# Both column halves of the second feed-forward product by seven-product slabs, two streams in the same seven PSUM banks

## The chip, the cores and the metric

One core of a Trainium2 chip runs the whole program in one launch. The metric is the device time of one execution in microseconds, as the median of several runs. The kernel before has 2032.6 us.

The engines are named as in the profile: PE multiplies matrices, PEld is its weight load, DVE does elementwise work with one or two tensor inputs, ACT does elementwise work with a function or a scale, POOL is a third elementwise engine that also issues DMAs, SP issues DMAs. SBUF is the on-chip memory of 128 partitions, PSUM the small accumulator memory that PE writes, in banks of 128 x 512 float32.

## What is computed

Two transformer layers over 256 tokens of width 2048, in float32. Each layer has a token mixer (pooling with memory attention in the first, differential attention with memory attention in the second) and a feed-forward block. The change is in the feed-forward block:

```python
def squared_relu_mlp(h, w1, w2):
    z = jax.nn.relu(h @ w1)
    return (z * z) @ w2
...
        x = x + squared_relu_mlp(rms_norm(x, ffn_norm[i]), w_ff1[i], w_ff2[i])
```

Here w1 is 2048 x 8192 and w2 is 8192 x 2048, so the second product sums over 8192 channels, 64 chunks of 128.

## The kernel before

**Precision.** A float32 operand is cut in two: a rounded part (hi, a cast by ACT) and the remainder (lo, a subtraction by DVE). A product of two such operands is three matmuls: hi by hi, hi by lo, lo by hi. Weights come from HBM in float32 and are cut on the way: `Feed._split` (L159) casts into `hi_ring` (L164) and subtracts into `lo_ring` (L165). The rings have six slots of 512 columns (`SLOTS`), and a slot is free again when PE has used it. Weights are prepared three jobs ahead of PE (`AHEAD`) and loaded three loads ahead of that (`LOADS`).

**Plain tiles.** `a_part` (L404) computes 128 output channels for all 256 tokens. For each 128 x 128 weight block it loads hi as PE's weights and streams 512 columns (the activations' hi and lo side by side, L418), then loads lo and streams 256 columns (L420). A tile over 16 chunks of k is 32 matmuls. Four blocks are a quad, one half of a 512 KB load (`raw`), and after each quad `tick()` runs the small work that was put off with `at(delay, ...)`.

**Slabs.** The right half of the second product's columns (1024 to 2047) goes by Winograd's form of Strassen's scheme: two chunks of k by two 512-column halves by two token halves of 128, in seven products where the plain way has eight. The seven products add into seven PSUM banks that stay open over the whole layer (`open_banks`, L848), and `finish_banks` (L853) forms the four result blocks and transposes them into the residual. A slab is four jobs (`slab_jobs`, L817; `sides` says which operands and banks): job 0 has two products, job 1 one, jobs 2 and 3 two each, 21 matmuls of 512 columns. Here the activations are PE's weights and the weight rows stream. The weight sums are made on DVE: `t1` (L192), then `rb` (L197), then `ra` (L189, 1024 columns). The activations' sums are made by `combine` (L748, L753 to L756) and cut into `sit` (L759, L762). A slab's rows are two loads of 512 KB (`slab`).

**The order of the feed-forward block.** `ffn` (L715) writes the order out by hand. Up tiles (first product, `up_tile`, L773) and down tiles (second product, left half, `down_tile`, L788) share one PSUM bank, `x_bank`; ACT copies it out (L739), DVE adds the two halves (L780) and multiplies the ReLU by the row scale r (one instruction at L781, shown at L314), ACT squares it (L784), ACT and DVE cut it into `z` (L743, L746). The 64 up tiles come in four quarters of 16; after each quarter 8 down tiles sum its 16 chunks into the residual (L799, L800), and 8 slabs take the same chunks. One slab goes to three tiles (`groups`), and its jobs stand between the tiles, so that PE has work while ACT copies `x_bank` out. The last four slabs and eight down tiles (`last`, L916) are mixed by the table `ends`.

**Loads.** All weight loads are issued by SP in the order of `Plan.loads`. For a slab, a preparing step ("K", two steps ahead of its first job, `KOFF`) makes the sums t1 and rb.

Of the kernel before, what the change touches and what calls it, by code (L numbers as in the profile page):

```python
# [17 lines left out]
P = 128  # L18
# [36 lines left out]
class Plan:  # L55
# [13 lines left out]
    def close(self):  # L69
        prep = []  # L70
        for job in self.jobs:

            late = job[0] == "S" and job[1] % 32 > 28
            if job[0] == "S" and job[2] == 0 and not late:
                prep.insert(max(0, len(prep) - KOFF), ("K", job[1]))
            if late and job[2] == 1:
                prep.append(("L", job[1]))
            prep.append(job)
# [4 lines left out]
        for p in prep:  # L83
            if p[0] == "K":
                self.loads += [("S", p[1], 0), ("S", p[1], 1)]
            elif p[0] == "L":
                self.loads.append(("S", p[1], 1))
            elif p[0] == "S" and p[2] == 0 and ("S", p[1], 0) not in self.loads:
                self.loads.append(("S", p[1], 0))
# [15 lines left out]
class Feed:  # L105


    def __init__(self, tc, wst, wpool, rows, plan, dry):
# [7 lines left out]
        self.t1 = None  # L116
        self.behind = None
# [7 lines left out]
    def load(self, upto):  # L125
        while self.lp < min(upto, len(self.plan.loads)):
# [6 lines left out]
            elif r[2] and r[1] % 32 > 29:  # L133
                t = self.spare[r[1] % 2]
            else:
                t = self.rows.tile([P, 1024], F32, tag="rows", bufs=3, name=f"slab{h}")
            self.nc.sync.dma_start(t[:, 0:n], self.wst[h, :, 0:n])
# [34 lines left out]
    def _prepare(self, p):  # L172
        sub, add = self.nc.vector.tensor_sub, self.nc.vector.tensor_add
        self.load(self.plan.need[p] + 1 + LOADS)
# [9 lines left out]
        t1 = self.t1[1 if p[1] % 32 > 28 else p[1] % 2]  # L184

        def both():
            t2 = rb[:, 0:512].unsqueeze(1).to_broadcast([P, 2, 512])
            two = ra.rearrange("p (a c) -> p a c", a=2)
            sub(two, t2, two)  # L189

        if p[0] in "KL":
            one = add(t1, ra[:, 0:512], rb[:, 0:512])  # L192
# [4 lines left out]
            sub(rb[:, 0:512], t1, rb[:, 512:1024])  # L197
            if p[0] == "L":
                both()
# [4 lines left out]
        if p[2] == 0 and ("K", p[1]) in self.plan.need:  # L204
            both()
# [71 lines left out]
def program(ctx, tc, plan, dry, xT, memT, par, lam, cst, wst, yT):  # L277
# [437 lines left out]
    def ffn(l, xs, tags, done):  # L715
# [8 lines left out]
        sit = sp.tile([P, 8, 1024], F32R, tag=tags[1], name=f"sit{l}")  # L724
        room = sp.tile([P, 6144], F32, tag="big", name=f"room{l}")
        stage = [room[:, T * j : T * j + T] for j in range(8)]
        sums = [room[:, 2048 + 512 * j : 2560 + 512 * j] for j in range(2)]

        feed.spare = [room[:, 1024 * j : 1024 * j + 1024] for j in range(2)]
        feed.t1 = [room[:, 3072 + 512 * j : 3584 + 512 * j] for j in range(2)]  # L730
        outs = [room[:, 4096 + 512 * j : 4608 + 512 * j] for j in range(3)]
        r = []
        banks = []
        cnt = [0]

        def evict(ps):
            x = outs[cnt[0] % 3]
# [4 lines left out]
        def high(j):  # L742
            nc.scalar.copy(z[:, j, 0:T], stage[j % 8])  # L743

        def low(j):
            nc.vector.tensor_sub(z[:, j, T : 2 * T], stage[j % 8], z[:, j, 0:T].bitcast(F32))  # L746

        def combine(i):  # L748

            a11, a21 = stage[2 * i % 8][:, 0:P], stage[2 * i % 8][:, P:T]  # L750
            a12, a22 = stage[(2 * i + 1) % 8][:, 0:P], stage[(2 * i + 1) % 8][:, P:T]
            s1, s2, s3, s4 = (sums[i % 2][:, c * P : c * P + P] for c in range(4))
            nc.vector.tensor_add(s1, a21, a22)  # L753
            nc.vector.tensor_sub(s3, a11, a21)
            nc.vector.tensor_sub(s2, s1, a11)
            nc.vector.tensor_sub(s4, a12, s2)  # L756

        def sums_high(i):
            nc.scalar.copy(sit[:, i, 0:512], sums[i % 2])  # L759

        def sums_low(i):
            nc.vector.tensor_sub(sit[:, i, 512:1024], sums[i % 2], sit[:, i, 0:512].bitcast(F32))  # L762

        def convert(j, d):
            at(d, lambda: high(j))
            at(d + 2, lambda: low(j))
            if j % 2:
                i = j // 2
                at(d + 3, lambda: combine(i))
                at(d + 5, lambda: sums_high(i))  # L770
                at(d + 7, lambda: sums_low(i))

        def up_tile(q, i, ps):  # L773
            a_part(ps, "w_ff1", l, q * NK + i, range(NK), xs)
            if not r:
                r.append(rstd_from("x"))
            y = evict(ps)

            def first():
                nc.vector.tensor_add(y[:, 0:T], y[:, 0:T], y[:, T : 2 * T])  # L780
                stt(y[:, 0:T], y[:, 0:T], 0.0, r[0], ALU.max, ALU.mult)  # L781

            at(1, first)
            at(3, lambda: nc.scalar.activation(stage[i % 8], y[:, 0:T], AF.Square))  # L784
            if q == 0 or i > 0:
                convert(i, 3)

        def down_tile(q, n, ps, between=None):  # L788
            end = l == 1 and q == 3 and n == 7
            if end:  # L790
                c_tile(ps, "w_ff2", l, n, range(q * NK, q * NK + NK), z)
                nc.vector.tensor_add(resid[:, n, :], resid[:, n, :], ps[:, 0:T])
# [692 lines left out]
```

## Time and profile before

| | before |
|---|---|
| median of 3 runs | 2032.6 us (2032.13 to 2032.81) |
| span of the profiled execution, first to last instruction | 2030.2 us |
| time of the profiled execution beside its span | not listed apart; the median lies 2.4 us above the span |
| ACT busy, in the stretch 600 to 800 us | 133.26 of 200 us |
| DVE busy, in the same stretch | 173.35 of 200 us |
| moved by DMA | 390.75 MB, mean 192 GB/s |
| granted clock of PE | 1.000 |

How to read it. In the list of groups a line shows the source line, the engine, the operation, output and inputs with their shapes, the count, the busy time in us and the mean duration in ns, then the idle time before these instructions and what ended it. A timeline row has the start, the duration, the engine and the instruction. The ends of matmuls are modelled, so their durations overlap; the pace of PE is read from start to start. A table of stretches has, for each, the length, the busy time of PE, PEld, DVE, ACT and POOL with the count of instructions, the granted clock, the share of the DMA engines and GB/s. The list of DMAs has the size and the time from issue to landing. The feed-forward block of the first layer runs from about 250 to 937 us, that of the second from about 1343 us to the end.

### The profile page before, as it was taken

To read this page: it belongs to the slowest core of one execution; us is meant where nothing else is said; L and a number is where in the kernel's file an instruction comes from. 1 tells how busy PE (TensorE), PEld (TensorE's weight loads), DVE (VectorE), ACT (ScalarE), POOL (GpSimd) and SP (SyncE) were. 2 spreads that over 40 slices of the span, in tenths; PEclk is the share of its full clock that TensorE was granted. 3 is DMA by queue.
4 is the path that set the end of the run, shared out by engine and by line. 5 is a ranking of instruction groups with operands and counts; after the bars stand their busy time and mean duration, and the time that the engine had idled before them with its cause. 6 is when DMAs were issued, how large, how long until landed. Compare 5 with 4: busy or idle time off the path is not lost.

```text
span 2030.2 us, 32210 instructions
## 1 busy us (share of the span) xinstructions
PE 2025.3 (100%) x11022; PEld 1744.0 (86%) x11022; DVE 1718.6 (85%) x3233; ACT 1352.6 (67%) x2537; POOL 53.5 (3%) x67
## 2 busy tenths in 40 slices
PE   9999999999999999999999999999999999999999
PEld 8888888888888888888888888888888888888888
DVE  8888889889879978999765798989879978888997
ACT  7765577666656756678665698566657656766764
POOL 0001300000000000000000000310000000000000
PEclk9999999999999999999999999999999999999999
DMA  9566556555556565655565534555555555565564
GB/s 318 167 201 190 191 176 204 191 197 198 187 198 203 185 205 195 206 178 178 187 235 191 173 122 155 188 180 200 187 198 198 187 204 194 188 213 195 193 209 135
DMA packets 110470, 390.75 MB, mean 192 GB/s; under 512 B 12512, under 2 KB 15200, under 8 KB 110304
## 3 DMA queue, kind: packets, MB, share of 16 engines
q1 hardware_dynamic: 110160, 388.68, 57.2%
q8 instruction: 86, 1.41, 0.3%
q14 instruction: 80, 0.66, 0.1%
q10 hardware_dynamic: 144, 0.01, 0.0%
HBM read 386.54 MB, written 2.10 MB: 191 GB/s over the span
## 4 chain that ended last, share of the span: by engine, by line
PE 99%; ACT 0%; DVE 0%; issue 0%
PE x_bank L418 33%; PE x_bank L420 16%; PE wo L418 6%; PE p L813 5%; PE p L814 5%; PE p L815 5%; PE wo L420 3%; PE u L418 2%; PE ff L418 2%; PE u L420 1%; PE q L452 1%; PE q L454 1%; PE k L452 1%; PE q L453 1%; PE k L454 1%; PE v L454 1%
## 5 line engine op out<-in xcount | busy, mean ns | idle before, releaser
L164 ACT CAST hi_ring<-raw 128x512 fp32r<-128x512 f32 x1193 | 736.0, 620 | 510.8 <-PE x_bank L418 302.9
L165 DVE TENSOR_TENSOR lo_ring<-raw,hi_ring 128x512 fp32r<-128x512 f32 x1193 | 816.2, 694 | 189.0 <-ACT hi_ring L164 148.9
L418 PE MATMUL x_bank<-fx,hi_ring 128*128 128x512 f32 x1920 | 601.8, 395 | 0.0
L420 PEld LDWEIGHTS x_bank<-fx,lo_ring 128*128 128x128 f32 x1920 | 360.6, 188 | 84.0
L420 PE MATMUL x_bank<-fx,lo_ring 128*128 128x256 f32 x1920 | 377.1, 278 | 0.0
L418 PEld LDWEIGHTS x_bank<-fx,hi_ring 128*128 128x128 f32 x1920 | 301.3, 189 | 9.4
L418 PE MATMUL x_bank<-z,hi_ring 128*128 128x512 f32 x960 | 300.9, 395 | 0.0
L165 DVE TENSOR_TENSOR lo_ring<-slab,hi_ring 128x1024 fp32r<-128x1024 f32 x188 | 229.9, 1223 | 54.2 <-ACT hi_ring L164 53.5
L164 ACT CAST hi_ring<-slab 128x1024 fp32r<-128x1024 f32 x188 | 196.8, 1047 | 73.3 <-PE x_bank L418 37.8
L420 PEld LDWEIGHTS x_bank<-z,lo_ring 128*128 128x128 f32 x960 | 180.3, 188 | 41.9
L420 PE MATMUL x_bank<-z,lo_ring 128*128 128x256 f32 x960 | 188.6, 278 | 0.0
L418 PE MATMUL wo<-cat,hi_ring 128*128 128x512 f32 x512 | 161.8, 397 | 0.3 <-DVE rc L389 0.3
L418 PEld LDWEIGHTS x_bank<-z,hi_ring 128*128 128x128 f32 x960 | 151.8, 189 | 6.4 <-ACT room L739 0.4
L420 PEld LDWEIGHTS wo<-cat,lo_ring 128*128 128x128 f32 x512 | 95.9, 188 | 22.0
L739 ACT COPY room<-x_bank 128x512 f32<-128x512 f32 x180 | 104.8, 582 | 2.0 <-PE x_bank L420 2.0
L420 PE MATMUL wo<-cat,lo_ring 128*128 128x256 f32 x512 | 101.5, 279 | 0.0
L813 PE MATMUL p<-hi_ring,sit 128*128 128x512 f32 x256 | 100.4, 392 | 0.0
L814 PE MATMUL p<-hi_ring,sit 128*128 128x512 f32 x256 | 100.1, 391 | 0.0
L815 PE MATMUL p<-lo_ring,sit 128*128 128x512 f32 x256 | 99.6, 389 | 0.0
L784 ACT ACTIVATE room<-room 128x256 f32<-128x256 f32 x128 | 53.2, 416 | 42.1 <-DVE room L314 41.9
L418 PEld LDWEIGHTS wo<-cat,hi_ring 128*128 128x128 f32 x512 | 78.3, 189 | 1.1 <-ACT mq L606 0.5
L813 PE MATMUL p<-hi_ring,z 128*128 128x512 f32 x192 | 75.1, 391 | 0.0
(343 smaller groups left out, 3078.2 us busy)
## 6 DMA issues: line engine op xcount, KB each, us to landing
raw<-in_w SPq DMA_DIRECT2D x596, 512.0 KB, 3.7
slab<-in_w SPq DMA_DIRECT2D x124, 512.0 KB, 3.6
memraw<-in_mem SPq DMA_DIRECT2D x5, 512.0 KB, 3.8
resid<-in_x SPq DMA_DIRECT2D x8, 256.0 KB, 5.6
room<-in_w SPq DMA_DIRECT2D x4, 512.0 KB, 5.0
out_y<-resid SPq DMA_DIRECT2D x16, 128.0 KB, 1.9
memraw<-in_mem SPq DMA_DIRECT2D x5, 256.0 KB, 5.6
memraw<-in_mem SPq DMA_DIRECT2D x2, 128.0 KB, 3.6
```

Of the source, the lines that this page charges most:

```text
L164: self.last_cast = self.nc.scalar.copy(hi, src)
L165: low = self.nc.vector.tensor_sub(lo, src, hi.bitcast(F32))
L418: nc.tensor.matmul(ps, hi, xs[:, k, :], start=first and c == 0, stop=False)
L420: nc.tensor.matmul(ps[:, T : 2 * T], lo, xs[:, k, 0:T], start=False, stop=last and c == len(ks) - 1,)
L452: nc.tensor.matmul(ps[t], x[t][1], hi, start=k == 0, stop=False)
L453: nc.tensor.matmul(ps[t], x[t][0], hi, start=False, stop=False)
L454: nc.tensor.matmul(ps[t], x[t][0], lo, start=False, stop=k == NK - 1)
L739: nc.scalar.copy(x, ps)
L784: at(3, lambda: nc.scalar.activation(stage[i % 8], y[:, 0:T], AF.Square))
L813: nc.tensor.matmul(ps, a[1], hi, start=first, stop=False)
L814: nc.tensor.matmul(ps, a[0], hi, start=False, stop=False)
L815: nc.tensor.matmul(ps, a[0], lo, start=False, stop=last)
```

## The change

1. The left half of the columns goes by slabs too, for the first 48 chunks of k: 24 more slabs in each layer. The last 16 chunks of the left half stay plain (8 down tiles).
2. There are now two streams, g = 0 (right half) and g = 1 (left half), for the same seven banks. The order is four slabs of one stream, then eight of the other, and so on. At each exchange the banks of one job are copied to SBUF by ACT, two ticks after that job's last product, and the other stream's partial sums are copied back into the bank by ACT (`swap`, `restore`); matmuls then add onto them. After the last slab of the left half its result blocks are formed at once (`close_left`) and transposed into the residual by four `turn_left`.
3. Up tiles run one after another from 4 to 63 with no down tiles between. `due` puts slab jobs before each tile and after each of its quads by a table of due times (`early`, `late`, even in between).
4. The row scale r is no longer applied in the up tile: ACT does ReLU and square, and r squared multiplies the results (`scale_rows`, four ACT instructions, and a DVE multiply per down tile). r squared as a column needs two more small matmuls per layer.
5. The sum t1 of two weight pieces is not added by DVE: one piece is loaded into `t1` (three buffers) and the other is added by a DMA with accumulation, issued by POOL. The first half of a slab's first row is so loaded twice.
6. z and sit become rings (16 chunks, 4 pairs): an entry is written when the slab that last used it is done (`when`). Buffers move (`room`, `big2`); `outs` has two buffers where it had three. Loads run four ahead in this part.

The core of the diff:

```diff
+            elif r[2] == 0:
+                t1 = r[1] % len(self.t1)
...
+                self.nc.sync.dma_start(self.t1[t1], self.wst[h, :, 0:512])
+                self.nc.sync.dma_start(t, self.wst[h])
+            else:
+                self.nc.gpsimd.dma_start(
+                    self.t1[r[1] % len(self.t1)], self.wst[h, :, 0:512], accum_op=ALU.add
+                )
+                self.nc.sync.dma_start(t[:, 512:1024], self.wst[h, :, 512:1024])
...
-        if p[0] in "KL":
-            one = add(t1, ra[:, 0:512], rb[:, 0:512])
+        if p[0] == "K":
+            one = sub(rb[:, 0:512], t1, rb[:, 512:1024])
...
-            sub(rb[:, 0:512], t1, rb[:, 512:1024])
...
-            def first():
-                nc.vector.tensor_add(y[:, 0:T], y[:, 0:T], y[:, T : 2 * T])
-                stt(y[:, 0:T], y[:, 0:T], 0.0, r[0], ALU.max, ALU.mult)
...
+            at(1, lambda: nc.vector.tensor_add(y[:, 0:T], y[:, 0:T], y[:, T : 2 * T]))
+            at(2, lambda: nc.scalar.activation(y[:, 0:T], y[:, 0:T], AF.Relu))
...
+        def restore(p, g):
+            if (g, p) in saved:
+                x = saved.pop((g, p))
+                nc.scalar.copy(banks[p], x)
+                keep.append(x)
+                back[p] = True
+            holds[p] = g
+
+        def swap(j, g):
+            for p in of_job[j]:
+                x = keep.pop(0)
+                nc.scalar.copy(x, banks[p])
+                saved[1 - g, p] = x
+                restore(p, g)
...
+        def close_left(j):
+
+            add, sub = nc.vector.tensor_add, nc.vector.tensor_sub
+            if j == 0:
+                left["u"], left["c11"] = keep.pop(0), keep.pop(0)
+                nc.scalar.copy(left["u"], banks[0])
+                add(left["c11"], left["u"], banks[1])
...
+        slabs = []
+        for h in range(6):
+            for g in (0, 1) if h % 2 == 0 else (1, 0):
+                slabs += [(g, 4 * h + i, g == h % 2) for i in range(4)]
+        slabs += [(0, i, False) for i in range(24, 32)]
...
+            if end and s + 1 < len(slabs):
+                if g == 1 and i == 23:
+                    at(1, lambda: close_left(j))
+                else:
+                    at(2, lambda: swap(j, 1 - g))
...
+        early = (4, 6, 8, 10, 11.5, 12.5, 13.5, 14.5, 15, 16, 17.5, 19, 20.5)
+        late = (58, 59.5, 61, 62.5, 64)
...
+        for i in range(4, 64):
+            due(i, 1)
+            if turns:
+                turn_left(turns.pop(0))
+                due(i, 1)
+            up_tile(i, bank(), lambda b, i=i: due(i + b / 16) if b > 0 and b % 4 == 0 else None)
```

`turn_left` makes four PE transposes of 128 x 128 into `x_bank`, has ACT copy the bank out and DVE add it to two chunks of the residual.

More of the change, by code (lines that the diff above doesn't have):

```diff
@@ L887, in ffn @@
         for i in range(4):
[L888 removed]
+            up_tile(i, mmt("ff1"))
         open_banks()
[L891 to L909 removed]
+        feed.loads_ahead = 4
@@ L912, in ffn @@
+        for i in range(4, 64):
[4 more added lines that the diff above has]
+            up_tile(i, bank(), lambda b, i=i: due(i + b / 16) if b > 0 and b % 4 == 0 else None)
+        due(64)
+        assert len(jobs) == 16 and not turns
+        feed.loads_ahead = LOADS
         ends = (
```

325 lines of the change are left out of this document (203 added, 122 removed).

## The prediction

> **What bounds the kernel now.** I read the page's busy times and its chain of work that ended last, then the list of waits of PE, then a table of stretches, and only then single instructions.
>
> ```profile
> PE 2025.3 (100%) x11022; PEld 1744.0 (86%) x11022; DVE 1718.6 (85%) x3233; ACT 1352.6 (67%) x2537; POOL 53.5 (3%) x67
> PE 99%; ACT 0%; DVE 0%; issue 0%
> PE warm L359 <- PEq L1458: 0.8, 1, 0.8
> PE st_mq L613 <- DVE mq_y L314: 0.3, 1, 0.3
> PE wo L418 <- DVE rc L389: 0.3, 1, 0.3
> ```
>
> PE is busy over the whole span, 99% of the chain is PE, and the list of PE's waits has three entries with 1.4 us in all. Busy PE alone proves little, so here is whether the feed-forward part runs at PE's own pace (columns: length, then busy PE, PEld, DVE, ACT, each with its count):
>
> ```profile
> 600.00:800.00 200.00, 200.00 (x1091) 172.48 (x1089) 173.35 (x302) 133.26 (x228) 0.00 (x0) 1.00 0.58 196
> 900.00:935.00 35.00, 35.00 (x194) 30.18 (x193) 33.22 (x57) 26.45 (x50) 0.00 (x0) 1.00 0.47 160
> ```
>
> The timeline of PE gives the two kinds of work. First a stretch of a plain tile, then of slab products:
>
> ```profile
> 902.04 0.62 PE L418 MATMUL x_bank<-z,hi_ring 128*128 128x512 f32 x2
> 902.73 0.63 PE L418 MATMUL x_bank<-z,hi_ring 128*128 128x512 f32 x2
> 903.43 0.40 PE L813 MATMUL p<-hi_ring,sit 128*128 128x512 f32 x1
> 919.41 0.40 PE L813 MATMUL p<-hi_ring,sit 128*128 128x512 f32 x1
> 921.46 0.39 PE L813 MATMUL p<-hi_ring,z 128*128 128x512 f32 x1
> ```
>
> From 902.04 to 903.43 PE works through four weight blocks of a plain tile: 0.3475 us a block, 5.56 us for a tile of 16. From 919.41 to 921.46 it issues nine slab products: 0.2278 us each, 4.78 us for the 21 of a slab, which also covers 16 weight blocks. Check: a round of 24 tiles and 8 slabs is 24 x 32 + 8 x 21 = 936 matmuls and 24 x 5.56 + 8 x 4.78 = 171.7 us, so 1090 in 200 us; the row from 600 to 800 has 1091. So PE never waits there, at a granted clock of 1.00, and in the row from 900 to 935 it kept pace while DVE was 95% busy.
>
> **The change part by part.**
>
> *PE.* Per layer 24 plain down tiles go (the left half for the first 48 chunks of k) and 24 slabs come. Both layers: 48 x (5.56 - 4.78) = 37.4 us less PE work. New on PE are 32 transposes of the left half (turn_left). Two like them from the timeline:
>
> ```profile
> 933.28 0.27 PE L878 MATMUL ct<-const,c_b 128*128 128x128 f32 x1
> 933.39 0.27 PE L878 MATMUL ct<-const,c_a 128*128 128x128 f32 x1
> ```
>
> They follow each other by 0.11 us: 32 x 0.11 = 3.5 us. The last tile gets one more DVE multiply, 0.4 us on the end. Without any new wait the span would be 2030.2 - 37.4 + 3.5 + 0.4 = 1996.7 us. Everything else depends on whether DVE and ACT still keep ahead of a faster PE.
>
> *DVE.* These are its groups (count | busy us, mean ns):
>
> ```profile
> L165 DVE TENSOR_TENSOR lo_ring<-raw,hi_ring 128x512 fp32r<-128x512 f32 x1193 | 816.2, 694 | 189.0 <-ACT hi_ring L164 148.9 <-PE p L814 26.8 <-PE v L453 2.0
> L165 DVE TENSOR_TENSOR lo_ring<-slab,hi_ring 128x1024 fp32r<-128x1024 f32 x188 | 229.9, 1223 | 54.2 <-ACT hi_ring L164 53.5 <-PE p L814 0.6
> L189 DVE TENSOR_TENSOR slab<-slab,slab 128x1024 f32<-128x1024 f32 x60 | 73.1, 1218 | 0.0
> L192 DVE TENSOR_TENSOR room<-slab,slab 128x512 f32<-128x512 f32 x60 | 41.9, 698 | 12.6 <-DMA slab<-in_w 12.3
> L197 DVE TENSOR_TENSOR slab<-room,slab 128x512 f32<-128x512 f32 x60 | 41.1, 685 | 0.0
> L314 DVE SCALAR_TENSOR_TENSOR room<-room,r_x 128x256 f32<-128x256 f32 x128 | 53.8, 420 | 0.7
> L780 DVE TENSOR_TENSOR room<-room 128x256 f32<-128x256 f32 x128 | 53.5, 418 | 1.2 <-ACT room L739 1.2
> L746 DVE TENSOR_TENSOR z<-room,z 128x256 fp32r<-128x256 f32 x128 | 53.5, 418 | 0.3
> L753 DVE TENSOR_TENSOR room<-room 128x128 f32<-128x128 f32 x64 | 18.4, 287 | 9.2 <-ACT room L784 9.2
> L762 DVE TENSOR_TENSOR sit<-room,sit 128x512 fp32r<-128x512 f32 x64 | 43.9, 686 | 0.7 <-ACT sit L759 0.7
> ```
>
> The add at L192 moves into an accumulating DMA, the multiply by r_x (L314) leaves the tile, and ReLU goes to ACT. What stays, by full durations: a tile needs 4 x 0.694 + 0.418 + 0.418 + 2 x 0.287 + 0.686 / 2 = 4.53 us; a slab 3 x 1.223 + 0.694 + 0.685 + 1.218 = 6.27 us. In the dense stretch the change puts 36 slabs over 37.5 tiles, 1.04 tiles to a slab. One such cycle costs PE 1.04 x 5.56 + 4.78 = 10.56 us and DVE 1.04 x 4.53 + 6.27 = 10.98 us, 104%. But instructions of DVE overlap at their ends:
>
> ```profile
> 605.28 0.68 DVE L165 TENSOR_TENSOR lo_ring<-raw,hi_ring 128x512 fp32r<-128x512 f32 x1
> 605.88 0.42 DVE L314 SCALAR_TENSOR_TENSOR room<-room,r_x 128x256 f32<-128x256 f32 x1
> 606.22 0.68 DVE L197 TENSOR_TENSOR slab<-room,slab 128x512 f32<-128x512 f32 x1
> 606.82 1.22 DVE L165 TENSOR_TENSOR lo_ring<-slab,hi_ring 128x1024 fp32r<-128x1024 f32 x1
> 607.96 0.69 DVE L165 TENSOR_TENSOR lo_ring<-raw,hi_ring 128x512 fp32r<-128x512 f32 x1
> ```
>
> From start to start 512 elements take 0.60 us, 256 take 0.34, 1024 take 1.14. At that pace a tile is 4 x 0.60 + 2 x 0.34 + 0.57 + 0.30 = 3.95 us, a slab 3 x 1.14 + 0.60 + 0.60 + 1.14 = 5.76 us, the cycle 9.87 us, 93% of PE's. I take this end: these rows are the very instructions, queued back to back. Sparser stretches (the first 12 slabs over 16.5 tiles, the end) lie lower. The Trainium skill, VectorE: DVE Perf Modes, section The DRAIN you can't avoid, says that the next instruction does not start until the pipe is empty; by that DVE would need its full durations. The trace disagrees: 0.60 us from start to start against a duration of 0.68.
>
> *ACT and the swaps.* Every eight slabs, four times a layer, all seven banks are copied out and seven others copied in; once before that only out, and once (close_left) left sums are formed. A copy into PSUM by ACT has no row; the bounds are the 0.58 us of a copy out of PSUM and the 0.62 of one within SBUF. I take 0.58.
>
> ```profile
> L164 ACT CAST hi_ring<-raw 128x512 fp32r<-128x512 f32 x1193 | 736.0, 620 | 510.8 <-PE x_bank L418 302.9 <-DVE lo_ring L165 59.6 <-PE wo L418 56.1
> L164 ACT CAST hi_ring<-slab 128x1024 fp32r<-128x1024 f32 x188 | 196.8, 1047 | 73.3 <-PE x_bank L418 37.8 <-PE p L814 33.9 <-PE ff L418 0.9
> L739 ACT COPY room<-x_bank 128x512 f32<-128x512 f32 x180 | 104.8, 582 | 2.0 <-PE x_bank L420 2.0
> L784 ACT ACTIVATE room<-room 128x256 f32<-128x256 f32 x128 | 53.2, 416 | 42.1 <-DVE room L314 41.9
> ```
>
> A cycle costs ACT 1.04 x (4 x 0.62 + 0.58 + 3 x 0.416 + 0.31) + 3 x 1.047 + 0.62 = 8.6 us of 10.56. A swap adds 14 x 0.58 = 8.1 us over little more than a cycle: 6.1 us too much. Behind each copy in ACT's queue stand the casts that DVE and then PE wait for. The neighbouring cycle has 2.0 us free, and the ring of six slots holds two jobs and two quads, 5.5 us of PE work, less the job in use (1.4) and DVE's split (1.2): 2.9 us. So 1.2 us of PE wait per full swap, 8 swaps, 10 us; the bounds are 0 and 6.1 each. PE reaches a swapped bank four jobs later, so the bank itself is ready. close_left adds seven DVE instructions of 512 elements (4.2 us at 0.60) and nine ACT copies in one cycle, of which DVE's 0.7 us of margin takes a part and the ring's lead most of the rest: 2 us each, 4 us in all (bounds 0 and 4.2 each). The four scalings that finish_banks adds cost nothing: two tiles of 5.56 us lie between them and the transposes that read them. Plain tiles share one bank, so the work between two tiles hides the copy out of it; in the program order of the changed kernel 40 of 139 such gaps are 0.91 or 1.14 us of PE work, where the kernel before has 1.37 at least. At 0.1 us each, 4 us (bounds 0 and 0.4 each). Together 18 us of waits.
>
> *DMA.* The operand that DVE added becomes one more 256 KB load and one 256 KB accumulating DMA from POOL's queue, which has nothing else to do in this part; an accumulation waits for its load, DVE's L193 waits for it, and behind that stand the splits. On SP's queue the extra load waits for one of three buffers that the slab before last has left, and the tiles' loads stand behind it. No row shows an accumulating DMA. Plain ones:
>
> ```profile
> slab<-in_w SPq DMA_DIRECT2D x124, 512.0 KB, 3.6
> room<-in_w SPq DMA_DIRECT2D x4, 512.0 KB, 5.0
> GB/s 318 167 201 190 191 176 204 191 197 198 187 198 203 185 205 195 206 178 178 187 235 191 173 122 155 188 180 200 187 198 198 187 204 194 188 213 195 193 209 135
> ```
>
> The load is issued when the slab before is prepared, a cycle (10.4 us) ahead. Load and accumulation at 3.6 to 5.0 us each are 7.2 to 10.0: hidden, barely at the upper end. Traffic in a dense cycle is 1.04 x 1.05 + 1.31 MB in 10.56 us, 227 GB/s; the first slice reached 318. I cost it at nothing; without cover each microsecond late costs one per slab.
>
> **Sum.** 1996.7 + 18 = 2014.7 us of span. The median of the runs (2032.6) lies 2.4 above this execution's span, so 2017 us.
>
> **The rivals.**
>
> (a) *No new waits at all*: 1996.7 + 2.4 = 1999 us. For it speaks PE's pace at 95% busy DVE; against it, that this lasted 35 us with no swap in it.
>
> (b) *DVE becomes the bound* (slower). If DVE cannot overlap as in the row above, because its waits on ACT and its own results come back to back, its 10.98 us per dense cycle replace PE's 10.56: 0.42 x 36 x 2 = 30 us, with the same 18 us on top: 1996.7 + 30 + 18 + 2.4 = 2047 us. It decides from the point where a DVE cycle exceeds 10.56 us. For it: 104% by durations. Against it: the start-to-start times.
>
> (c) *POOL slows DVE.* The trace has DVE instructions with POOL at work beside them:
>
> ```profile
> L314 DVE SCALAR_TENSOR_TENSOR fx<-resid,param,fx 128x256 fp32r<-128x256 f32 x32 | 27.4, 858 | 0.0
> L314 DVE SCALAR_TENSOR_TENSOR mems<-memraw,param,mems 128x256 fp32r<-128x256 f32 x32 | 14.5, 478 | 1.6 <-ACT mems L396 1.6
> ```
>
> The same operation takes 0.38 us more. If each of the 112 DMAs from POOL held up two DVE instructions so, a cycle would be 9.87 + 0.76 = 10.63 us: DVE has no margin left and each swap costs 4.1 us instead of 1.2, giving 2017 + 23 = 2040 us. The Trainium skill, SBUF — State Buffer, section Who interferes with whom, says that a DVE instruction with two SBUF inputs contends with a GpSimd instruction that reads SBUF but not with one that only writes, and infers that descriptor generation needs the write side; by that, nothing is added. The fx row agrees for reads; no run so far shows it for a DMA.
>
> (d) *The accumulation is late.* If it took 10 us, the chain would be 13.6, 3 us late in each of some 72 dense slabs: over 2200 us.
>
> **How the numbers follow.** Forecast (waits of 8 to 27 us, 2007 to 2026): 0.48. (a), 1998 to 2007: 0.22. (b): 0.13, (c): 0.10, (d): 0.03; 0.04 for waits in between that end within 0.2% (2028.5 to 2036.7), about what a measurement of this kernel can tell from no change. Half of (c) and a little of (b) falls in that band too: same 0.10, slower 0.20, faster 0.70. The range from 1999 to 2046 leaves out (d), the upper half of (b) and the edge of (a).
>
> **What would show it.** Right: PE still 99% of the chain; dense cycles near 10.6 us; PE's list of waits holding 10 to 30 us, at ACT's casts near the copies of p; DVE above 90% busy there. Rival (b): PE waits on lo_ring in every cycle, not only near swaps. (c): DVE durations above 0.69 beside the DMAs. (d): DVE idle at L193. Wrong outright: PE's slab products slower than 0.228 us from start to start.

## The result and the profile after

The changed kernel takes 2059.7 us (median of four runs, 2053.3 to 2064.4) beside 2032.4 for the kernel before (2032.0 to 2032.8): ratio 1.0132, 95% interval 1.0114 to 1.0151. It is slower, and the forecast of 2017 us (range 1999 to 2046) was wrong. The profiled execution took 2058.8 us, its span is 2057.0. Its runs spread over 11 us where those of the kernel before spread over 0.8.

From the page of the changed kernel, the busy times and the chain that ended last, and then its list of waits of PE (engine, line, tile, what it waited for: us in all, times, longest):

```profile
PE 2017.2 (98%) x10534; PEld 1702.6 (83%) x10534; DVE 1760.9 (86%) x3089; ACT 1501.2 (73%) x2791; POOL 149.9 (7%) x179
PE 89%; DMA 3%; DVE 3%; ACT 3%; issue 1%; DVEq 0%; POOL 0%; SPq 0%; ACTq 0%
PE p L847 <- DVE lo_ring L172: 16.1, 15, 3.6
PE tc_x L488 <- DVE rs_t L316: 13.5, 2, 7.0
PE x_bank L420 <- ACT room L748: 2.0, 4, 0.7
```

PE has 488 matmuls fewer, as planned, but it is 89% of the chain instead of 99%, and DMA, DVE and ACT have come into it. The two big waits are on DVE: slab products that wait for a low half (lo_ring), and tc_x, the two small matmuls for the column of r squared (x4 in the profile), which I had not priced at all. What did DVE itself wait for?

```profile
DVE lo_ring L172 <- ACT hi_ring L171: 160.1, 270, 1.6
DVE room L193 <- DMA room<-in_w: 30.9, 26, 3.5
DVE slab L193 <- DMA slab<-in_w: 19.1, 13, 4.2
DVE slab L193 <- DMA room<-in_w: 11.9, 2, 6.0
```

The first line was longer in the kernel before (203.2 us at its L165). New are the other three: 62 us at L193, the step that makes `rb`'s lower half as t1 minus its upper half ("the combining step" from here), always for a DMA. In the kernel before, the corresponding first instruction waited 12.3 us.

Which DMA was it? The view of a source line lists who waited for its DMAs (us, times). First L144, the plain load of `rb`'s upper half by SP, then L141, the accumulating DMA by POOL:

```profile
  DVE room L193: 29.5, 24
  DVE slab L193: 19.1, 13
```

```profile
  DVE slab L193: 11.9, 2
  DVE room L193: 1.5, 2
```

So 37 of the 41 waits (48.6 of 61.9 us) were for the plain load. The accumulation ended four (13.4 us), all of them in the first two slabs of a feed-forward block.

The timeline of DVE and SP of the changed kernel shows one such wait, and below it the timeline of PE at that place (start, length, instruction; in brackets the idle time before it and what ended it):

```profile
1806.49 1.22 DVE L172 TENSOR_TENSOR lo_ring<-room,hi_ring 128x1024 fp32r<-128x1024 f32 x1
1807.74 0.33 SPq L144 DMA_DIRECT2D room<-in_w  x1
1809.89 0.29 DVE L783 TENSOR_TENSOR room<-stage,room 128x128 f32<-128x128 f32 x1
1813.40 0.69 DVE L193 TENSOR_TENSOR room<-room 128x512 f32<-128x512 f32 x1 [3.22 <-DMA room<-in_w]
1814.01 2.35 DVE L172 TENSOR_TENSOR lo_ring<-slab,hi_ring 128x1024 fp32r<-128x1024 f32 x2
```

```profile
1811.98 0.39 PE L844 MATMUL p<-hi_ring,z 128*128 128x512 f32 x1
1815.28 0.50 PE L847 MATMUL p<-lo_ring,sit 128*128 128x512 f32 x1 [2.91 <-DVE lo_ring L172]
1815.62 0.55 PE L846 MATMUL p<-hi_ring,z 128*128 128x512 f32 x1
1815.96 0.63 PE L847 MATMUL p<-lo_ring,z 128*128 128x512 f32 x1
1816.39 1.06 PE L420 MATMUL x_bank<-fx,hi_ring 128*128 128x512 f32 x2
1819.27 0.40 PE L846 MATMUL p<-hi_ring,z 128*128 128x512 f32 x1
```

The load of `rb`'s upper half goes out at 1807.74, as soon as the split at 1806.49 has left the single buffer `spare` (1806.49 + 1.22 = 1807.71). So it is with each load into `spare` within a layer: it goes out 0.03 us after the end of the split that used the buffer last. The combining step is at the head of DVE's queue from 1810.2 on (1809.89 + 0.29) and waits until 1813.4. This slab's accumulation had landed at 1802.7. Right behind the step stand two splits of 1024 columns, the last of the slab two before the step's own and the first of the slab before it, which do not need this transfer. PE reaches those splits at 1812 and stands for 2.9 us. Then it runs on at 0.34 to 0.43 us a matmul instead of 0.23 until about 1819.

The start of the feed-forward has the same pattern. DVE's and then PE's timeline:

```profile
258.25 0.42 DVE L805 TENSOR_TENSOR room<-room 128x256 f32<-128x256 f32 x1
264.71 0.69 DVE L193 TENSOR_TENSOR slab<-room,slab 128x512 f32<-128x512 f32 x1 [6.04 <-DMA room<-in_w]
265.82 0.69 DVE L193 TENSOR_TENSOR room<-room 128x512 f32<-128x512 f32 x1 [0.42 <-DMA room<-in_w]
266.43 0.42 DVE L316 SCALAR_TENSOR_TENSOR rs_t<-st_x,rs_t 128x256 f32<-128x256 f32 x1
```

```profile
266.90 1.01 PE L488 MATMUL tc_x<-ones_d,acc 128*128 128x2 f32 x4 [6.50 <-DVE rs_t L316]
267.77 1.20 PE L420 MATMUL ff<-fx,hi_ring 128*128 128x512 f32 x2
```

Two combining steps stand ahead of `rs_t`, which reads the bank that tc_x needs. So the shared bank makes PE wait, but what it waits for is once more the combining step.

**A tally of PE.** A busy PE is modelled, so I went through its timeline and summed up by how much each interval from start to start exceeds the pace of its kind (0.469 us for a pair of L420, 0.115 for one of L422, 0.228 for a slab product), where it is over 0.05 us. For the changed kernel that gives 9.7 and 9.5 us at the two feed-forward starts (250 to 300 and 1340 to 1400 us) and 17.1 and 21.7 us in the dense stretches (300 to 950 and 1400 to 2020): 58.0 us. In the kernel before it is below 1 us. My 1996.7 us without waits plus 58.0 is 2054.7, 2.3 short of the span. The waits explain the loss; the listed ones are little more than half of it, because the list leaves out short gaps and the slow matmuls after a long one.

**The clock.** Windows of PE in the changed kernel (length, busy PE, granted clock, DMA share, GB/s):

```profile
260.00:267.00 7.00, 0.50 (x4) 0.69 0.73 128
267.00:273.00 6.00, 6.00 (x21) 0.51 0.57 135
273.00:280.00 7.00, 7.00 (x43) 1.00 0.38 140
603.40:605.40 2.00, 0.82 (x4) 1.00 0.24 38
605.40:609.00 3.60, 3.60 (x19) 1.00 0.89 223
```

After 6.5 us without work the clock is 0.51 for about 5 us; after 1.2 us without work at 603.4 it stays at 1.00. The Trainium skill, TensorE: Matmul & The Clock Gate, section What's actually happening, says that the clock falls to half after an idle window of some 3.4 us and comes back after as long a time of work; the trace agrees for these two stalls, with some 5 us until the clock was back. The long one costs half as much again as it lasts (9.7 us of tally for 6.5 us of waiting). Two stalls shorter than the rule's window disagree, and there the measurement decides: after the 2.9 us at 1812 the granted clock was 0.55 from 1815.3 to 1819.0, and a stall of 1.8 us in e3 (below) was followed by a lower clock as well:

```profile
1339.00:1343.00 4.00, 3.47 (x16) 0.73 0.26 70
```

### The profile page after: what moved, and what is told of

Same layout as the page of the kernel before. It is cut to its first block, busy times and chain, and to the rows that moved or that the text cites. A ratio compares the mean times of both kernels' runs of the same rounds, so it can differ in the third digit from the quotient of the medians.

```text
span 2057.0 us, 31770 instructions
## 1 busy us (share of the span) xinstructions
PE 2017.2 (98%) x10534; PEld 1702.6 (83%) x10534; DVE 1760.9 (86%) x3089; ACT 1501.2 (73%) x2791; POOL 149.9 (7%) x179
## 4 chain that ended last, share of the span: by engine, by line
PE 89%; DMA 3%; DVE 3%; ACT 3%; issue 1%; DVEq 0%; POOL 0%; SPq 0%; ACTq 0%
PE x_bank L420 21%; PE x_bank L422 11%; PE p L847 8%; PE p L844 8%; PE p L846 8%; PE wo L420 6%; PE wo L422 3%; DVE lo_ring L172 2%; PE u L420 2%; DMA room<-in_w 2%; PE ff L420 2%; ACT hi_ring L171 1%; DMA slab<-in_w 1%; PE u L422 1%; PE q L454 1%; PE q L456 1%
## 5 line engine op out<-in xcount | busy, mean ns | idle before, releaser
L171 ACT CAST hi_ring<-raw 128x512 fp32r<-128x512 f32 x1001 | 614.5, 620 | 281.4 <-PE x_bank L420 75.5
L172 DVE TENSOR_TENSOR lo_ring<-raw,hi_ring 128x512 fp32r<-128x512 f32 x1001 | 687.0, 694 | 113.7 <-ACT hi_ring L171 103.0
L420 PE MATMUL x_bank<-fx,hi_ring 128*128 128x512 f32 x1920 | 606.8, 397 | 2.0 <-ACT room L748 2.0
L422 PEld LDWEIGHTS x_bank<-fx,lo_ring 128*128 128x128 f32 x1920 | 361.5, 188 | 84.0 <-DVE lo_ring L172 1.7
L172 DVE TENSOR_TENSOR lo_ring<-slab,hi_ring 128x1024 fp32r<-128x1024 f32 x280 | 340.5, 1221 | 58.6 <-ACT hi_ring L171 55.2
L422 PE MATMUL x_bank<-fx,lo_ring 128*128 128x256 f32 x1920 | 378.8, 279 | 0.8 <-DVE lo_ring L172 0.8
L171 ACT CAST hi_ring<-slab 128x1024 fp32r<-128x1024 f32 x280 | 292.4, 1048 | 101.5 <-PE x_bank L420 60.8
L420 PEld LDWEIGHTS x_bank<-fx,hi_ring 128*128 128x128 f32 x1920 | 318.1, 189 | 45.6 <-ACT room L748 18.2
L847 PE MATMUL p<-lo_ring,sit 128*128 128x512 f32 x448 | 177.0, 396 | 12.8 <-DVE lo_ring L172 12.5
L141 POOL DMA_DIRECT2D room<-in_w x112 | 96.9, 868 | 1183.5 <-DMA room<-in_w 1163.1
L844 PE MATMUL p<-hi_ring,sit 128*128 128x512 f32 x448 | 177.5, 396 | 1.3 <-ACT hi_ring L171 1.3
L846 PE MATMUL p<-hi_ring,sit 128*128 128x512 f32 x448 | 175.9, 393 | 0.0
L420 PE MATMUL wo<-cat,hi_ring 128*128 128x512 f32 x512 | 161.8, 397 | 0.3 <-DVE rc L391 0.3
L171 ACT CAST hi_ring<-room 128x512 fp32r<-128x512 f32 x168 | 128.5, 765 | 38.1 <-PE p L846 15.6
L172 DVE TENSOR_TENSOR lo_ring<-room,hi_ring 128x512 fp32r<-128x512 f32 x168 | 144.8, 862 | 1.9 <-ACT hi_ring L171 1.9
L847 PE MATMUL p<-lo_ring,z 128*128 128x512 f32 x336 | 132.0, 393 | 3.7 <-DVE lo_ring L172 3.7
L844 PE MATMUL p<-hi_ring,z 128*128 128x512 f32 x336 | 132.0, 393 | 0.2
L846 PE MATMUL p<-hi_ring,z 128*128 128x512 f32 x336 | 131.8, 392 | 0.0
L422 PEld LDWEIGHTS wo<-cat,lo_ring 128*128 128x128 f32 x512 | 95.9, 188 | 22.0
L422 PE MATMUL wo<-cat,lo_ring 128*128 128x256 f32 x512 | 101.5, 279 | 0.0
```

The lines of the kernel that those rows point to most:

```text
L141: self.nc.gpsimd.dma_start(self.t1[r[1] % len(self.t1)], self.wst[h, :, 0:512], accum_op=ALU.add)
L171: self.last_cast = self.nc.scalar.copy(hi, src)
L172: low = self.nc.vector.tensor_sub(lo, src, hi.bitcast(F32))
L420: nc.tensor.matmul(ps, hi, xs[:, k, :], start=first and c == 0, stop=False)
L422: nc.tensor.matmul(ps[:, T : 2 * T], lo, xs[:, k, 0:T], start=False, stop=last and c == len(ks) - 1,)
L844: nc.tensor.matmul(ps, a[1], hi, start=new, stop=False, **again)
```

## The experiments

Theory: DVE's queue is in order, and the scheduler that orders each engine's instructions has put the combining step ahead of splits that are ready, further than the loads allow. Rivals: DVE simply has too much to do; the accumulating DMA itself is too slow; the column matmuls and their shared bank are a cost of their own. "Lead" below is the time from a combining step to the subtraction that first uses its result (L205), a median over the 112 slabs; in e3 and e6 it counts from the addition, which there comes first.

| kernel | time, us | ratio to before (95%) | DVE idle at L193 for DMA, us | lead, us (a tenth above) | tally of PE, us |
|---|---|---|---|---|---|
| changed | 2059.7 | 1.0132 (1.0114 to 1.0151) | 61.9 | 9.2 (16.3) | 58.0 |
| e1 columns later | 2051.3 | 1.0079 (1.0053 to 1.0105) | 61.4 | 9.5 (15.8) | 50.1 |
| e2 step held | 2009.9 | 0.9890 (0.9875 to 0.9905) | 0 | 4.9 (5.9) | 9.5 |
| e3 sum on DVE | 2018.4 | 0.9927 (0.9912 to 0.9942) | 7.4 | 7.6 (11.2) | 15.0 |
| e4 = e1 + e2 | 2009.2 | 0.9887 (0.9873 to 0.9902) | 0 | 4.9 (5.9) | 9.3 |
| e5 = e2, no swap copies | 2006.0 | 0.9871 (0.9856 to 0.9886) | 0 | 4.9 (6.1) | 6.1 |
| e6 = e2 + e3 | 2012.3 | 0.9903 (0.9886 to 0.9919) | 0 | 5.3 (6.0) | 11.0 |
| e7 before, step held | 2032.2 | 1.0000 (0.9990 to 1.0009) | | | |
| e8 first slab held | 2051.8 | 1.0095 (1.0080 to 1.0110) | 49.2 | 8.8 (15.8) | 48.9 |
| e9 first two slabs held | 2031.4 | 0.9996 (0.9981 to 1.0010) | 31.5 | 8.7 (15.7) | 29.3 |
| e10 held loosely | 2013.3 | 0.9907 (0.9892 to 0.9923) | 12.5 | 7.7 (9.2) | 12.7 |
| e11 loads six ahead | 2052.4 | 1.0112 (1.0088 to 1.0136) | 53.7 | 9.6 (16.5) | 46.6 |
| e12 = e4, two jobs a gap | 2003.7 | 0.9859 (0.9843 to 0.9876) | 0.2 | 5.9 (6.9) | 6.5 |

Lead, idle time and tally are of the profiled execution. Between the changed kernel and e2, the tally falls by 48.5 us and the span by 48.7.

**e1: the columns elsewhere.**

```diff
                 r.append(rstd_from("x"))
-                r.append(columns("x")[1])
                 nc.scalar.activation(r[0], r[0], AF.Square)
+            if i == 2: r.append(columns("x")[1])
```

> Edit: the two column matmuls and their chain (the r-squared column) are called in the third up tile instead of the first; nothing else. In the changed kernel TensorE stands 6.5 us and 7.0 us at tc_x, because st_x and tc_x share one bank and the second waits for the whole rsqrt chain of the first, and after each of the two stalls the matmuls run at half pace for about 5 us (matmul pair 0.85 us in place of 0.47). Theory (the stall costs its length and the slow matmuls after it): both FFN starts get back 9.5 us, 19 us in all, 2040 to 2042 us. Rival 1 (the slow matmuls are something of the FFN start itself): 13.5 us, 2046. Rival 2 (the wait only moves, to the first of the next tiles): under 5 us, 2055 or more.

8.4 us came back, not 19; the time lies between the numbers of the two rivals. The tc_x wait is gone from PE's list, but another has come in its place at the next matmul that needs a split, 10 us of tally at the two starts (changed kernel: 19.2):

```profile
PE p L847 <- DVE lo_ring L172: 20.0, 19, 3.5
PE ff L422 <- DVE lo_ring L172: 3.6, 2, 2.2
```

The theory as I had put it (the columns are a cost of their own) was wrong: DVE stands as before, and only the first victim is another.

**e2: the combining step held.** An order rule without any semaphore; DVE's work stays the same.

```diff
-        self.split[job] = (hi, lo, range(a, a + n))
+        self.split[job], self.last_low = (hi, lo, range(a, a + n)), low.ins.name
...
             one = sub(rb[:, 0:512], t1, rb[:, 512:1024])
+            self.order(one, self.last_low)
```

> Edit: an order-only rule holds each slab's combining step (rb lower half = t1 - rb upper half) behind the last low-half split emitted before it; the scheduler had moved it ahead, in places by most of a slab. No wait or transfer is changed. Theory (late loads in an in-order queue): VectorE stood 62 us at this step waiting for DMA with splits behind it that were ready, and nearly every stall of TensorE over 0.5 us in the dense stretches comes 1 to 8 us behind such a wait; held back, the loads have landed: that idle falls under 20 us, TensorE's loss in the dense stretches from 39 us to about 15, time 2033 to 2040. Rival (VectorE's load): the work in a cycle is the same 9.9 of 10.6 us, so the stalls reappear at the splits: 2055 to 2065.

It took 2009.9 us (2009.75 to 2010.08), 50 us less than the changed kernel and more than the theory had dared: I had counted the starts as a separate cost, and they went as well. The list of PE's waits of e2, whole, and two of DVE's groups (busy, mean ns | idle before):

```profile
PE p L844 <- ACT hi_ring L171: 1.1, 2, 0.5
PE warm L361 <- PEq L1604: 0.8, 1, 0.8
PE st_mq L615 <- DVE mq_y L316: 0.3, 1, 0.3
PE wo L420 <- DVE rc L391: 0.3, 1, 0.3
```

```profile
L193 DVE TENSOR_TENSOR slab<-room,slab 128x512 f32<-128x512 f32 x56 | 38.5, 688 | 0.0
L193 DVE TENSOR_TENSOR room<-room 128x512 f32<-128x512 f32 x56 | 38.5, 687 | 0.0
```

No wait is left at L193, and none of PE's on lo_ring. The hold moves more than the step, though: some 220 of DVE's other 2977 instructions stand at other places in its order. The cleaner pairs are e8 and e9 below. Nothing about the transfers has changed; all three kinds of 256 KB transfer still land as late after their issue. First the DMA rows of the changed kernel (KB each, median us to landing), then those of e2:

```profile
room<-in_w SPq DMA_DIRECT2D x168, 256.0 KB, 3.3
room<-in_w POOLq DMA_DIRECT2D x112, 256.0 KB, 5.9
slab<-in_w SPq DMA_DIRECT2D x56, 256.0 KB, 4.5
```

```profile
room<-in_w SPq DMA_DIRECT2D x168, 256.0 KB, 3.2
room<-in_w POOLq DMA_DIRECT2D x112, 256.0 KB, 5.9
slab<-in_w SPq DMA_DIRECT2D x56, 256.0 KB, 4.3
```

And DVE does more in the same time, not less. The stretch from 600 to 800 us in the changed kernel, then in e2 (busy PE, PEld, DVE, ACT, POOL, each with its count):

```profile
600.00:800.00 200.00, 194.17 (x981) 160.52 (x980) 179.92 (x269) 160.00 (x272) 15.52 (x18) 1.00 0.73 216
```

```profile
600.00:800.00 200.00, 199.46 (x1017) 166.41 (x1016) 188.70 (x280) 161.42 (x274) 16.12 (x19) 1.00 0.76 225
```

My dense cycle of 10.56 us holds 1.04 x 32 + 21 = 54.3 matmuls, 1028 in 200 us. The changed kernel made 981, e2 1017.

**e3: the sum back on DVE, no accumulating DMA.**

```diff
-                self.nc.sync.dma_start(self.t1[t1], self.wst[h, :, 0:512])
...
-                self.nc.gpsimd.dma_start(
-                    self.t1[r[1] % len(self.t1)], self.wst[h, :, 0:512], accum_op=ALU.add
-                )
-                self.nc.sync.dma_start(t[:, 512:1024], self.wst[h, :, 512:1024])
+                self.nc.sync.dma_start(t, self.wst[h])
...
+            one = add(t1, ra[:, 0:512], rb[:, 0:512])
-            one = sub(rb[:, 0:512], t1, rb[:, 512:1024])
+            sub(rb[:, 0:512], t1, rb[:, 512:1024])
```

> Edit: the sum t1 = lower half of ra + lower half of rb is made by VectorE as before the change, both rows loaded whole by one load each; no accumulating DMA, no t1 load. Everything else of the change stays. Adds 112 additions at 0.60 us start to start, 67 us of VectorE, 9.87 to 10.47 us in a cycle of 10.56; takes 29 MB of accumulating and 29 MB of plain loads away, and 112 DMAs from SP. Theory (late loads): the VectorE idle at the combining step falls from 62 to about 12 us, as in the kernel before, and pays for most of the added work: 2050 to 2065. Rival (VectorE's load bounds): the stalls grow by most of what no slack is left for, 30 to 60 us: 2090 to 2120. Second rival (the accumulating DMA alone is what was late): below 2045.

2018.4 us, better than my theory's 2050 and inside the second rival's bound: without the accumulating DMA the loss is mostly gone. But two things have moved together. The transfers are fewer, and the lead is shorter (7.6 us for 9.2), since the scheduler arranged DVE anew. e3 alone can't say which counts; e6 and e10 say more, and by the list of waits above the accumulating DMA of the changed kernel was late only at the two starts. What it shows is that 67 us more of DVE work did not hurt, against the rival of a DVE with too much to do.

**e4: e1 and e2 together.**

> Edit: e1 and e2 together. Theory: the two costs are apart in time and add: 19 + 20 to 25 us less, 2015 to 2021, faster than the kernel before (2032.4). Rival (VectorE's load): 2036 to 2046, only the columns' part. If the two share something (the same late loads at the start of the feed-forward), the sum is 5 us short.

2009.2 us, 0.7 less than e2. The costs do not add, because they were one cost.

**e5: e2 without the swaps' copies.** ACT's copies in `restore` and `swap` are left out.

> Edit on top of e2 (combining step held): the ACT copies of the swaps, from bank to SBUF and back, are left out, 140 copies back and those out of the bank in the swaps, so both halves are summed up in one bank and the second feed-forward product's result is not the reference's. Theory (the swaps hide behind TensorE): TensorE's trace in e2 shows two waits on ACT of 0.54 us where swaps stand, 0.81 us each with what follows: 1 to 3 us less than e2, 2007 to 2009. Rival (the prediction's term, 8 swaps at 1.2 us and 18 us of waits in all, hidden in gaps too short to be listed): 10 us less, 2000.

2006.0 us: the 140 ACT copies (70 into banks, 70 out of them; the expectation counted them wrongly) cost 3.9 us in all, a little more than I had read from the trace and far less than the 10 us of the prediction.

**e6: e2 and e3 together.**

> Edit: e2 and e3 together: the sum t1 on VectorE instead of the accumulating DMA, and the combining (now add and subtract) held behind the last low-half split emitted before it. Theory (with the step in its place the accumulating DMA saves VectorE time that TensorE does not need): 2009 to 2016, no more than 6 us behind e2, since the prediction's cycle of VectorE then is 10.47 of 10.56 us, just under the bound. Rival (VectorE bounds as soon as it is at 99% of the cycle): 2025 to 2040. e3 without the hold took 2018.4.

2012.3 us, 2.4 more than e2. DVE's row in the same stretch:

```profile
600.00:800.00 200.00, 199.17 (x1015) 165.64 (x1014) 196.44 (x297) 160.82 (x272) 0.00 (x0) 1.00 0.61 200
```

At 98% busy DVE still keeps PE at 1015 matmuls in 200 us. So DVE's load is not the bound, and part 5 of the change, the accumulating DMA, is worth 2.4 us where the step is held. Where it is not held, taking that DMA away and the shorter lead that came with it are worth 41 us together (e3).

**e7: the control.** The kernel before, its combining step held by the same lines.

> Edit: the kernel before, with its combining step (add, then subtract) held in the same way. Control: if the hold only repairs what the change brought, the kernel before, in which TensorE has no listed wait in the feed-forward, keeps its 2032.2 us within 1 us. If the hold is a gain for itself, it falls by 5 us or more; if it makes splits late, it rises.

2032.2 us, ratio 1.0000: the hold is no gain for itself. Without the hold, DVE of the kernel before waits for loads at this step too (12.3 us), but PE has no listed wait in its feed-forward.

**e8 and e9: only the first slabs held.**

```diff
+            if p[1] % 56 == 0: self.order(one, self.last_low)   # e8
+            if p[1] % 56 < 2: self.order(one, self.last_low)    # e9
```

> Edit: the changed kernel, the combining step held for the first slab of each feed-forward only, the other 110 placed by the scheduler as in the changed kernel. Theory (the 6.5 and 7.0 us at tc_x are the rsqrt chain's VectorE steps queued behind this step, which waits 6 us for the first accumulating DMA): both stalls at the FFN start go, 15 to 19 us with the slow matmuls after them, the dense stretches keep their 39 us: 2041 to 2045. Rival (the shared bank makes the stall): the stalls stay, 2058. e1, which moved the column matmuls away instead, took 2051.3 and showed the stall at the next matmul that needed a split, 3.6 us.

2051.8 us; the expectation failed, and so did the rival's number. DVE's timeline of e8 shows why:

```profile
257.70 0.42 DVE L805 TENSOR_TENSOR room<-room 128x256 f32<-128x256 f32 x1
265.31 0.69 DVE L193 TENSOR_TENSOR room<-room 128x512 f32<-128x512 f32 x1 [7.18 <-DMA room<-in_w]
265.92 0.42 DVE L316 SCALAR_TENSOR_TENSOR rs_t<-st_x,rs_t 128x256 f32<-128x256 f32 x1
```

With slab 0's step held, slab 1's stands in its place before `rs_t`, and its data come later still.

> Edit: the changed kernel, the combining step held for the first two slabs of each feed-forward only. In e8 (first slab held) the second slab's step stood in the same place, ahead of the rsqrt chain's rs_t, and waited 7.2 us; e8's expectation failed there. Theory: with both held the stalls at tc_x go (6.8 and 6.9 us in e8, 9.3 and 10.1 with the slow matmuls after them): 19 us under e8, 2031 to 2036, or by the changed kernel's 2059.7 less its 19 us, 2041: 2031 to 2041. Rival (another step of a later slab takes the place, or the bank's sharing makes the stall after all): 2046 or more.

2031.4 us (2025.0 to 2040.5): both stalls at the starts go from 19.4 us of tally in e8 to 1.3, and the column matmuls stand in the first tile as in the changed kernel. So the shared bank alone costs next to nothing. In DVE's order only the four held steps and one other instruction have moved against the changed kernel, and 28 us came back. The time left above e2, 21.5 us, is the price of the dense stretches, where all 31.5 us of e9's waits at L193 are for the plain load of the upper half and none for the accumulation. The spread of 15 us between executions of e9, beside 0.3 in e2, points the same way: the four kernels without a listed wait at L193 (e2, e4, e5, e6) spread by 0.1 to 1.6 us. It is no measure of the waits, though: e8 has more of them than e9 and spreads by 4.8 us.

**e10: how far ahead is too far.**

```diff
-            self.order(one, self.last_low)
+            self.order(one, self.lows[-4])
```

> Edit: as e2, but the combining step is held behind the fourth last low-half split emitted before it, not the last, so the scheduler may move it ahead of up to three splits. In the changed kernel the step runs a median 9.2 us ahead of the subtraction that uses it (a tenth of them 16.4 us or more), in e2 4.9 us. Theory (how far ahead of ready splits the step stands, against transfers that land at a given time, decides): a lead between the two, 6 to 8 us, and a time between them, 2012 to 2035, with VectorE's DMA waits at the step between 0 and 62 us. Rival (only the start of the feed-forward or only the far outliers matter): as e2 within 2 us.

2013.3 us at a lead of 7.7: between e2 and the changed kernel, near e2. The DMA waits rise from 0 at 4.9 us to 12.5 at 7.7 and 61.9 at 9.2 with its long tail. The rival (as e2 within 2 us) fails: e10 is 3.4 us above e2.

**e11: loads earlier, no hold.** `feed.loads_ahead = 6` in place of 4. In 16 places the row buffer of the odd slabs is then refilled before the earlier slab's rows have been split, so part of the second product is summed from other rows than the reference's; the loads, the sums and their number stay.

> Edit: the changed kernel with its loads emitted six entries ahead in place of four, no hold. Theory (the transfers of the late slabs wait in SP's queue for buffers that a split of an earlier slab frees, so emitting them earlier doesn't start them earlier): the DMA waits of the combining step stay at 50 us or more and the time within 10 us of the changed kernel, 2050 to 2070. Rival (loads are emitted too late): the waits fall under 25 us, 2015 to 2040. The order of VectorE changes with it, which may shift either by some us.

2052.4 us, DMA waits 53.7: as the theory has it. Emitting a load earlier does not make it land in time where the buffer is what it waits for. Since DVE's order changed too, this is weaker evidence than the others.

**e12: what was left.** e4's two edits and

```diff
-            due(i, 1)
+            due(i, 2 if i > 12 else 1)
             if turns:
```

> Edit on top of e4 (columns later, combining step held): from up tile 13 on at least two slab jobs, not one, stand between two plain tiles, so that PE has 1.37 us of work or more while ACT copies the shared bank out. In e2's trace 24 tiles in the dense stretch of one layer start with a first matmul pair of 0.52 to 0.57 us in place of 0.47, 2.2 us a layer, and PE's weight load is listed as waiting 72 times for that copy. Theory (the narrow gaps make these): 3 to 5 us less than e4's 2009.2, 2004 to 2006. Rival (the gaps are from something else, or the bunched jobs make splits late): 2009 or more.

2003.7 us (2003.65 to 2004.24), the best of all, 28.8 us under the kernel before. Who waited for the shared bank, in e4 and then in e12:

```profile
  PEld x_bank L420: 16.4, 72
```

```profile
  PEld x_bank L420: 2.0, 9
```

## Why the prediction was wrong, point by point

- **The step that failed** is the paragraph on DMA, which watched one transfer and took the place of the step for granted: "The load is issued when the slab before is prepared, a cycle (10.4 us) ahead. Load and accumulation ... 7.2 to 10.0: hidden, barely at the upper end ... I cost it at nothing". The size of that chain was right in sum: 3.2 us (the t1 loads by themselves) + 5.9 = 9.1 us, though 5.9 alone is above the 5.0 allowed. But the chain was not what came late. By the timelines of the changed kernel, the t1 load goes out a median of 22.0 us ahead of the combining step, not 10.4, and the accumulation has landed 22.6 us ahead of the first use (L205), 16.3 at the least. What came late, in 37 of 41 waits, is the plain load of `rb`'s upper half, for which the prediction has no term: it waits for its buffer, goes out a median of 16.0 us and lands 12.5 us ahead of the use (6.6 at the least). The row of L192 that the prediction shows had a sign of it, 12.3 us of waits for a slab's load. And the step itself, which I took to stand where the program emits it (two steps ahead of the slab's first job), stands in the order that runs on DVE a median of 9.2 us ahead of its use, and 16 us in a tenth of the slabs. In e2 the same load lands as far ahead (12.6 us, 5.5 at the least), but the step stands at 4.9 and finds it there. Cost: 48.5 us of tally, e2 against the changed kernel.
- **Rival (d)** named the place ("DVE idle at L193"), with a chance of 0.03, for an accumulation that is a full 3 us late in every dense slab. The place was right and the transfer was not: of the 41 waits (62 us of DVE, 58 us of PE with what follows a stall) only four were for the accumulation. Thinking that lateness must hit each slab alike also made it look too dear to be likely. Some slabs had slack and some had none.
- **The column of r squared** was left out of the sum. In the changed kernel it takes the two longest stalls of PE (13.5 us together), but e2 and e9 show that it is only the first in line behind the combining step.
- **PE's gain** was right. In e2 the span is 2008.3 us and the tally of waits 9.5, so 1998.8 without them, against 1996.7 forecast.
- **The 18 us of other waits** were too much in sum, and not alike. Swaps: 10 forecast, 3.9 measured (e5); in e2's list stand two waits of 0.5 us on ACT, so the ring's lead hides nearly all. The copy into a bank had no row before; it has one now, 604 ns in the median for 56 of the 70 and 586 for the others (the 0.58 taken was close). `close_left`: 4 forecast; in e2 no interval of PE over 0.3 us falls near it. Gaps of the shared bank: 4 forecast, 5.5 measured (e12 against e4).
- **DVE** (93% of the cycle from start to start): right. Between 300 and 950 us, DVE of e2 is 93% busy by the row below, and e6 runs at 98%. So rival (b), a DVE that becomes the bound, is refuted: that its 2047 us is the nearest number to the result is luck. The section of the Trainium skill that the prediction cites on DVE's pace adds that a next instruction which is not held starts earlier, so the early starts contradict the sentence quoted and not the section as a whole.

```profile
300.00:950.00 650.00, 649.46 (x3344) 546.95 (x3343) 605.64 (x954) 518.27 (x898) 43.98 (x51) 1.00 0.73 218
```

- **Rival (c)**, POOL's DMAs slowing DVE: refuted. The low-half group of the changed kernel has the mean that it had before, with 112 DMAs issued by POOL beside it, and the 88 of its instructions that run beside one of these have a mean of 683 ns:

```profile
L172 DVE TENSOR_TENSOR lo_ring<-raw,hi_ring 128x512 fp32r<-128x512 f32 x1001 | 687.0, 694 | 113.7 <-ACT hi_ring L171 103.0 <-PE v L455 2.0 <-PE tr L587 1.6
```

That is what the Trainium skill, SBUF — State Buffer, section Who interferes with whom, infers for DMAs issued by GpSimd: the trace agrees.

What stays open: why the dense stretches of e9 lose less than those of the changed kernel (28 us of tally for 39) with the same order there but for two slabs; the executions of both spread by over 10 us, so one profile each does not settle it. That a second row buffer for the odd slabs would also cure the waits was not tried. Nor does any run show why the scheduler put the step so far ahead.

## What to carry to other kernels

When a change makes an instruction of an in-order engine wait for transfers, read that instruction's place in the order that runs, not in the order in which the program emits it, and count from that place whether each of its transfers has landed: the plain loads that wait for a buffer as well as the new kind of DMA. In this case the scheduler had put the instruction ahead of work that was ready. The remedy to try first is to hold the instruction back, which cost nothing here (e2, e7), before buffers are added or the transfer is taken out. And when executions of one kernel begin to differ by some 10 us where they agreed within 1, look for an engine that waits for DMAs.

## What the runs showed of the hardware

- A 256 KB accumulating DMA issued by POOL lands 5.9 us after its issue in the median (3.6 to 9.0), a plain load of the same size issued by SP (t1) 3.2 us (2.5 to 8.6). POOL is busy 0.87 us for each.
- ACT copies 128 x 512 from SBUF into a PSUM bank in 0.60 us, about as fast as out of it (0.58), and matmuls add onto the copied sums.
- A stall of PE costs more than its length if it is long: 6.5 us of waiting became 9.7 us of tally at a granted clock of 0.51; after 2.9 us the clock was 0.55, after 1.8 us (e3) 0.73 from 1339 to 1343 us, and 1.2 us at 603.4 left it at 1.00.
- DVE sustains 98% busy over 200 us, counted with overlapping ends, without PE's pace falling (e6).
